# Token-major residual: down, output, v and embedding-gate products with 512 moving weight columns

## The chip, the cores and the metric

The kernel runs on one core of one Trainium2 chip. The metric is the device time of one execution in microseconds (us). TensorE (PE) multiplies; VectorE (DVE) and ScalarE (ACT) do elementwise work; GpSimd (POOL) does a few powers; SyncE (SP) issues most transfers from memory.

## The reference

256 tokens of width 1024 go through two blocks A and then two blocks B. A SwiGLU network has 2816 hidden columns. All arithmetic is fp32.

```
# block A, twice
h = h + 0.5 * swiglu(rmsnorm(h, g1), w_gate, w_up, w_down)
z = rmsnorm(h, g2) @ w_in          # MLA, differential attention, pooling, 3 gates
h = h + sum(sigmoid(z_gate) * (branches @ w_branch)) @ w_out
h = h + 0.5 * swiglu(rmsnorm(h, g3), w_gate, w_up, w_down)
# after both: h = rmsnorm(h, final_norm)
# block B, twice: each step ends in a norm of its own before the residual
h = h + rmsnorm(swiglu(rmsnorm(h, ..), ..), ln_ffn1_post)
h = h + rmsnorm([attention | mLSTM | RWKV](rmsnorm(h, ..)) @ w_out, ln_mix_post)
h = h + rmsnorm(swiglu(rmsnorm(h, ..), ..), ln_ffn2_post)
h = h + rmsnorm(sigmoid(rmsnorm(h, ..) @ w_ple_gate) * (ple @ w_ple_proj), ln_ple_post)
```

## The kernel before

The residual `x` is kept feature-major: 128 partitions of features, 8 chunks of them, 256 tokens. An fp32 product is made of three passes over operands split in two parts each (`hi`, `lo`): hi·hi, hi·lo and lo·hi (`mm3`, L330). The stationary operand is a 128x128 piece of weight, the moving one 256 columns of tokens. Gate and up (`mm2`, L337) take hi and lo of the activation as one moving operand of 512 columns and then 256 more. `weights` (L291) fetches a weight of 512 KB into one of four `raw` buffers in two pieces; ACT makes the hi part in slices of 128x512 (L449) and DVE the lo part (L450). The weights of the next stage are fetched and split "ahead" while the last down product runs.

An FFN (`ffn`, L688) walks over 11 groups of 256 hidden columns: gate, up, silu, product, split into `h`, and the down product of the group before into four PSUM banks `acc`. A norm at the start of a step (`Norm`, L509) doesn't scale the activation: it splits `x` times the gain into hi and lo (L452, L453), sums the squares with ACT, DVE and a product with ones (L422), takes a power -0.5 on POOL, spreads the factor over partitions with a matmul (L430), and the factor is multiplied in behind the products (`rb`). In A, `x` is updated bank by bank as the last down product's banks end (L776, L778). In B a norm lies between the product and the residual (`Post`, L586): the sum of squares over all features must be known before any of `x` can be updated, so `finish` (L641) comes after the last product: column sums (L601), the power, the spread, then the multiplies and adds chunk by chunk (L663, L666), each followed by the split for the next product. `warm` (L434) puts 7 and 8 bf16 matmuls of zeros (L438) beside this chain.

A scheduler orders the instructions of every engine from the program and modelled durations; `chain` (L311) pins a few of them one behind the other. Each engine runs its own list strictly in order. The lines of the profile:

```
L334 mm3: one of three passes, 256 moving columns     L341/L342 mm2: 512 and 256 columns
L449/L450 split of weights or h (ACT hi / DVE lo)      L452/L453 split of x times a gain
L438 warm   L430 spread   L422/L601 column sums        L415/L656 power on POOL
L663/L666 residual update in B   L776/L778 residual update in A   L1740, L1741, L1744 embedding gate
```

## Time and profile before

| | |
|---|---|
| median of 3 runs | 2453.72 us (2452.12 to 2458.3) |
| the profiled execution | 2454.61 us |
| its span | 2452.8 us |
| PE busy / DVE / ACT / POOL | 2401.3 / 1855.1 / 1474.5 / 43.6 us |
| mean granted clock of PE | 0.991 |

Busy time is the time in which an engine had an instruction under way. A matmul's duration contains the length of the pipeline, so that neighbours overlap: what one costs in a stream is the distance from its start to the next one's start, not its duration. All times below are on one axis that begins with the span. PEclk is the share of full speed that PE was granted in a stretch: 1.00 is 2.4 GHz, and a stretch that lies half at 1.2 GHz reads 0.75.

### The profile page before, as it was taken

What the parts mean: (1) busy time and instruction counts of PE and PEld (TensorE: products, weight loads), DVE (VectorE), ACT (ScalarE), POOL (GpSimd) and SP (SyncE); (2) the same over time, 40 slices, a digit from 0 to 9 for tenths busy, and PEclk for the clock granted to TensorE, in tenths of its full rate; (3) what the DMA queues carried; (4) which work ended last, traced back from release to release, by engine and by line L of the source; (5) the groups of instructions that cost most, each with busy time, mean ns of one, the idle gap of its engine ahead of it and who ended that gap; (6) DMA issues with size and microseconds to landing.
All of it is one profiled execution on the core that took longest, in us unless ns stands there. A gap on an engine that the chain in (4) does not pass through costs nothing. (4 is left out here: it accounts for less than half of the span.)

```text
span 2452.8 us, 45590 instructions
## 1 busy us (share of the span) xinstructions
PE 2401.3 (98%) x17164; PEld 2234.8 (91%) x17164; DVE 1855.1 (76%) x3620; ACT 1474.5 (60%) x2954; POOL 43.6 (2%) x43
## 2 busy tenths in 40 slices
PE   8999999999999999999999999999989999999998
PEld 7999999999999999999999988989989998898997
DVE  7667888767767888877787688777667768877765
ACT  6556765656656676566666663466666665346655
POOL 0000000000000000000000000000000000000000
PEclk9999999999999999999999999999999998999998
DMA  6554444555555444455555542156525554215651
GB/s 227 187 187 155 147 143 167 189 190 189 184 191 190 143 147 148 166 197 189 181 189 185 185 135 83 44 170 212 199 95 194 187 180 132 84 43 165 214 198 58
DMA packets 110510, 396.62 MB, mean 162 GB/s; under 512 B 12752, under 2 KB 13264, under 8 KB 110288
## 3 DMA queue, kind: packets, MB, share of 16 engines
q1 hardware_dynamic: 109008, 391.33, 47.7%
q8 instruction: 135, 2.21, 0.3%
q10 hardware_dynamic: 1280, 2.36, 0.3%
q14 instruction: 87, 0.71, 0.1%
HBM read 392.60 MB, written 1.05 MB: 160 GB/s over the span
## 5 line engine op out<-in xcount | busy, mean ns | idle before, releaser
L449 ACT ACTIVATE wh<-raw 128x512 fp32r<-128x512 f32 (+1 forms) x1446 | 891.6, 628 | 456.0 <-PE mm L334 120.0
L450 DVE TENSOR_TENSOR wl<-raw,wh 128x512 fp32r<-128x512 f32 (+1 forms) x1446 | 978.8, 688 | 239.5 <-ACT wh L449 218.6
L341 PE MATMUL mm<-act,wh 128*128 128x512 f32 x1728 | 613.2, 395 | 13.4 <-ACT wh L449 8.8
L342 PE MATMUL mm<-act,wl 128*128 128x256 f32 x1728 | 482.2, 280 | 0.7 <-DVE wl L450 0.7
L334 PE MATMUL acc<-h,wh 128*128 128x256 f32 x2560 | 457.0, 280 | 0.0
L334 PE MATMUL mm<-act,wh 128*128 128x256 f32 (+1 forms) x2176 | 422.5, 289 | 7.4 <-DVE sc L890 2.5
L341 PEld LDWEIGHTS mm<-act,wh 128*128 128x128 f32 x1728 | 324.3, 188 | 86.0 <-ACT wh L449 8.8
L334 PEld LDWEIGHTS acc<-h,wh 128*128 128x128 f32 x2560 | 391.2, 188 | 4.1 <-ACT h L449 0.3
L334 PE MATMUL acc<-h,wl 128*128 128x256 f32 x1280 | 355.8, 279 | 0.0
L334 PEld LDWEIGHTS mm<-act,wh 128*128 128x128 f32 (+1 forms) x2176 | 342.7, 190 | 13.9 <-ACT act L452 3.3
L342 PEld LDWEIGHTS mm<-act,wl 128*128 128x128 f32 x1728 | 326.2, 189 | 1.8 <-DVE wl L450 1.2
L334 PE MATMUL mm<-act,wl 128*128 128x256 f32 x1088 | 310.9, 287 | 0.0
L341 PE MATMUL up<-act,wh 128*128 128x512 f32 x832 | 296.0, 394 | 0.1
L334 PEld LDWEIGHTS acc<-h,wl 128*128 128x128 f32 x1280 | 240.5, 188 | 0.3
L342 PE MATMUL up<-act,wl 128*128 128x256 f32 x832 | 232.2, 279 | 0.0
L334 PEld LDWEIGHTS mm<-act,wl 128*128 128x128 f32 x1088 | 206.6, 190 | 2.6 <-issue 1.8
L341 PEld LDWEIGHTS up<-act,wh 128*128 128x128 f32 x832 | 155.9, 187 | 34.1 <-DVE uu L349 0.5
L342 PEld LDWEIGHTS up<-act,wl 128*128 128x128 f32 x832 | 156.8, 189 | 0.5
L348 ACT ACTIVATE jn<-mm 128x256 f32<-128x256 f32 x216 | 80.2, 372 | 88.7 <-PE mm L342 88.6
L743 ACT ACTIVATE ga<-ga 128x512 f32<-128x512 f32 x88 | 55.1, 630 | 100.6 <-DVE ga L742 100.6
L349 DVE TENSOR_TENSOR ga<-mm,jn 128x256 f32<-128x256 f32 x112 | 47.1, 421 | 65.8 <-ACT jn L348 65.8
L341 PE MATMUL acc<-act,wh 128*128 128x512 f32 x256 | 92.4, 401 | 1.9 <-ACT wh L449 1.9
(506 smaller groups left out, 3242.0 us busy)
## 6 DMA issues: line engine op xcount, KB each, us to landing
raw<-a_wgate SPq DMA_DIRECT2D x88, 512.0 KB, 4.3
raw<-a_wup SPq DMA_DIRECT2D x88, 512.0 KB, 4.0
raw<-a_wdown SPq DMA_DIRECT2D x88, 512.0 KB, 4.3
raw<-b_wgate SPq DMA_DIRECT2D x88, 512.0 KB, 4.6
raw<-b_wup SPq DMA_DIRECT2D x88, 512.0 KB, 4.5
raw<-b_wdown SPq DMA_DIRECT2D x88, 512.0 KB, 4.4
raw<-a_win SPq DMA_DIRECT2D x80, 512.0 KB, 3.7
raw<-a_wbr SPq DMA_DIRECT2D x24, 512.0 KB, 3.6
```

What stands on the lines that cost most here:

```text
L334: pin(s.nc.tensor.matmul(out, lhsT=w[x], rhs=a[:, y], start=start and i == 0, stop=stop and i == 2, skip_group_check=True))
L341: s.nc.tensor.matmul(bank, lhsT=hi, rhs=a.rearrange("p a t -> p (a t)"), start=start, stop=False, skip_group_check=True)
L342: s.nc.tensor.matmul(bank[:, :T], lhsT=lo, rhs=a[:, 0], start=False, stop=stop, skip_group_check=True)
L348: s.nc.scalar.activation(t, b[:, T:], AF.Copy)
L349: s.nc.vector.tensor_tensor(out[:, i], b[:, :T], t, op=ALU.add)
L449: pin(nc.scalar.activation(hi, src, AF.Copy))
L450: pin(nc.vector.tensor_tensor(lo, src, hi.bitcast(F32), op=ALU.subtract))
L743: nc.scalar.activation(ga, ga, AF.Silu)
```

## The change

`x` becomes token-major: 128 tokens on partitions, two halves, 1024 features. For down, both `w_out`, the v columns, the embedding gate and its projection the operands change places: 128 tokens of the activation are stationary, and 512 columns of weight (384 for the v columns of B) move (`yt`, `gemm_h`). The same holds for the first group of each FFN, whose gate and up weights now lie side by side in one 512-column weight; its `h` comes out token-major and is transposed back on PE. All other products are as before. For them the norm transposes `x` on PE, four 128x128 pieces to a PSUM bank, and splits each piece from PSUM (`Norm.cols`). Sums of squares are now along a row: one ACT instruction with an accumulator for each token half. The norm factor is a value per partition, so that the residual update is one DVE instruction per 512 columns. In B the gain is a tile `G` of 128 equal rows, fetched for each step. The last down product runs the four banks of half 0 and 1 in order of halves. `warm`, the column sums and the third weight fetched ahead go.

```diff
+    def yt(s, out, w, c, n, a, h, start, stop, pin=lambda i: i):
+        w = w.cols(c, n)
+        for i, (x, y) in enumerate(((0, 0), (1, 0), (0, 1))):
+            pin(s.nc.tensor.matmul(out, lhsT=a[:, y, h * P:h * P + P], rhs=w[x], start=start and i == 0, ...
+    def gemm_h(s, ws, act, tags, both=False):
+        for i in range(2 * 8):
+            h, k = (i % 2, i // 2) if both else (i // 8, i % 8)
+            w, p = parts[k]
+            s.yt(bs[h][:, :w.m], w, p * w.m, w.m, act[k], h, k == 0, k == 7)
 class Norm:
+    def cols(n, h, q):
+        b = s.ps(n.tags[q])
+        for i in range(4):
+            k = 4 * q + i
+            s.nc.tensor.transpose(b[:, i * P:(i + 1) * P], s.x[:, h, k * P:(k + 1) * P], s.c("ident"))
+        for i in range(4):
+            s.split(a[:, 0, ts], a[:, 1, ts], b[:, i * P:(i + 1) * P], n.gain[:, k:k + 1])
+    def square(n, h):
+        s.nc.scalar.activation(s.tile([P, D], "sj"), s.x[:, h], AF.Square, scale=D ** -0.5, accum_out=ss)
+    def factor(n, h):
+        n.power(n.r[:, h:h + 1], n.var[:, h:h + 1], n.square(h))
 class Post:
-        s.warm("up", 7)
-        rb = s.spread_ps(r, s.chain)
-            s.warm("up", 8)
+    def bank(p, h, q, y, half):
+        s.nc.scalar.activation(s.tile([P, D], "sj")[:, :512], y, AF.Square, scale=..., accum_out=p.ss[h][:, q:q + 1])
+        s.nc.vector.tensor_tensor(p.yg[h][:, c], y, p.G[:, c], op=ALU.mult)
+    def finish(p, h, eps, nxt, out=None):
+        nc.vector.scalar_tensor_tensor(v, ss[:, 0:1], eps ..., ss[:, 1:2], op0=ALU.add, op1=ALU.add)
+        nc.gpsimd.tensor_tensor(r, v, s.mhalf[:, :1], op=ALU.pow)
+        for q in range(2):
+            nc.vector.scalar_tensor_tensor(s.x[:, h, c], p.yg[h][:, c], r, s.x[:, h, c], op0=ALU.mult, op1=ALU.add)
+            if nxt is not None:
+                nxt.cols(h, q)
+        if nxt is not None:
+            nxt.factor(h)
 def ffn(...)
+        for hf, i, kk in ([(hf, i, kk) for hf in range(2) for i in range(2) for kk in range(2)] if last else
+                          [(hf, i, kk) for kk in range(2) for i in range(2) for hf in range(2)]):
+            s.yt(acc[hf][i], w, kk * D + i * 512, 512, h[:, kk], hf, j == 0 and kk == 0, last and kk == 1, ...
         if j == 0:
-            g, u, g2 = s.gemm2([wg[j], wu[j], wg[1]], act, ("mm", "mm", "acc", "acc", "acc", "acc"), ws=ws)
+            bs = s.gemm_h(ws or [s.weights([w])[0] for w in wgu], act, ("mm", "mm"), first)
+            for hf in range(2):
+                nc.scalar.activation(ga, bs[hf][:, :T], AF.Silu, scale=nrm.r[:, hf:hf + 1])
+                nc.vector.tensor_tensor(ht, bs[hf][:, T:], ga, op=ALU.mult)
+                for kk in range(2):
+                    nc.tensor.transpose(two(b)[:, kk, o], ht[:, kk * P:(kk + 1) * P], s.c("ident"))
+                s.split(h[:, :, 0, o], h[:, :, 1, o], two(b)[:, :, o])
 def mix_a(...)
+    for h, b in enumerate(s.gemm_h(ws, act, ("mm", "mm"))):
+        nc.scalar.activation(vd[:, h], b, AF.Copy, scale=nrm.r[:, h:h + 1])
```

How the instructions move is shown at three places. The first is PE's list at the end of the second FFN of A's first layer; before, the last down product (`dh`, `dl` are its weights) is followed by the gate product of the next FFN (`wh`, `wl`):

```order
L334 MATMUL acc_5905<-h_7647,dh_7734 128x256 x2
L334 MATMUL acc_5905<-h_7647,dl_7735 128x256
L341 MATMUL mm_7909<-act_7824,wh_7750 128x512 [waits DVE_49,PE_49]
L342 MATMUL mm_7909<-act_7824,wl_7751 128x256
L341 MATMUL mm_7910<-act_7824,wh_7750 128x512 [waits PE_49]
L342 MATMUL mm_7910<-act_7824,wl_7751 128x256
```

After, the same place (`st` and `up` are the PSUM banks that take the transposed `x`):

```order
L416 MATMUL acc_5505<-dh_7094,h_6906 128x512
L544 MATMUL st_7165<-cst_63,x_61 128x128 [waits DVE_49]
L544 MATMUL st_7165<-cst_63,x_61 128x128 x3
L544 MATMUL up_7180<-cst_63,x_61 128x128 [waits DVE_49]
L544 MATMUL up_7180<-cst_63,x_61 128x128 x3
L416 MATMUL mm_7243<-wh_7102,act_7170 128x512 [waits Activation_49]
L416 MATMUL mm_7243<-wl_7103,act_7170 128x512
L416 MATMUL mm_7243<-wh_7102,act_7170 128x512 [waits DVE_49]
L416 MATMUL mm_7243<-wh_7106,act_7170 128x512 [waits Activation_49]
```

Eight transposes of token half 0 stand between the last down product and the next stage's first, which waits for a split made from them; another eight, of half 1, stand further down among the products of half 0. The second place is ACT's list there; before, splits straight from `x` stand among the squares:

```order
L452 ACTIVATE act_7824<-x_61,vec_62 128x256 [waits DVE_49]
L452 ACTIVATE act_7824<-x_61,vec_62 128x256
L526 ACTIVATE sq_7829<-x_61 128x512
L452 ACTIVATE act_7824<-x_61,vec_62 128x256 [waits DVE_49]
L452 ACTIVATE act_7824<-x_61,vec_62 128x256
```

After, the same splits come from PSUM, in alternation between the two banks (`act_7170` and `act_7185` are the two halves of the features):

```order
L554 ACTIVATE sj_7195,v_1644_7194<-x_61 128x1024 [waits DVE_49]
L471 ACTIVATE act_7170<-st_7165,vec_62 128x128 [waits PE_49]
L554 ACTIVATE sj_7228,v_1648_7227<-x_61 128x1024 [waits DVE_49,Activation_49]
L471 ACTIVATE act_7185<-up_7180,vec_62 128x128 [waits PE_49]
L471 ACTIVATE act_7170<-st_7165,vec_62 128x128 [waits DVE_49]
L471 ACTIVATE act_7185<-up_7180,vec_62 128x128 [waits DVE_49]
```

The square of token half 1 stands behind the first split, and each later split waits for DVE's lo part of the one before from the same bank. The third place is PE's list at the end of the first FFN group of that next FFN, after the change (`jn` is the token-major product of silu(gate) and up; before there is no such transpose):

```order
L416 MATMUL mm_7244<-wl_7135,act_7185 128x512
L416 MATMUL mm_7244<-wh_7134,act_7185 128x512 [waits DVE_49]
L674 MATMUL up_7293<-cst_63,jn_7295 128x128 x2
L352 MATMUL mm_7337<-act_7170,wh_7320 128x512 [waits PE_49,Activation_49]
L674 MATMUL up_7293<-cst_63,jn_7303 128x128 [waits DVE_49]
L674 MATMUL up_7293<-cst_63,jn_7303 128x128
L353 MATMUL mm_7337<-act_7170,wl_7321 128x256 [waits DVE_49]
```

One product of the next group stands between the last product of half 1 and the transpose that needs its silu and multiply.

## Rows read from the trace of the kernel before

**Rows 1.** page: busy us (share of the span) and instructions of each engine

```profile
PE 2401.3 (98%) x17164; PEld 2234.8 (91%) x17164; DVE 1855.1 (76%) x3620; ACT 1474.5 (60%) x2954; POOL 43.6 (2%) x43
```

**Rows 2.** timeline of PE in A's first mixer: start us, us, what

```profile
242.03 0.28 PE L334 MATMUL mm<-act,wl 128*128 128x256 f32 x1
...
242.75 0.40 PE L377 MATMUL S<-wh,qm 128*128 128x512 f32 x1
...
243.45 0.28 PE L334 MATMUL mm<-act,wl 128*128 128x256 f32 x1
```

**Rows 3.** timeline of PE, A layer 1, first FFN to mixer

```profile
799.32 0.40 PE L334 MATMUL acc<-h,dh 128*128 128x256 f32 x2
...
805.07 0.51 PE L334 MATMUL mm<-act,wh 128*128 128x256 f32 x3
```

**Rows 4.** timeline of PE, A layer 0: the spread in its mixer

```profile
221.05 0.60 PE L430 MATMUL st<-cst,r 128*128 128x128 f32 x4
```

**Rows 5.** waits of PE over the whole span: us, times, longest

```profile
PE mm L334 <- DVE ud L1166: 3.4, 2, 1.9
PE mm L334 <- DVE sc L890: 2.5, 2, 1.2
```

**Rows 6.** groups of ACT by form: count, busy us, mean ns, idle before

```profile
L743 ACT ACTIVATE ga<-ga 128x512 f32<-128x512 f32 x88 | 55.1, 630 | 100.6 <-DVE ga L742 100.6
...
L861 ACT ACTIVATE pT<-PT 128x128 f32<-128x128 f32 x16 | 4.3, 270 | 2.0 <-PE PT L859 1.4 <-ACT sc L849 0.3
...
L946 ACT ACTIVATE qk<-row 32x1024 f32<-32x1024 f32 x4 | 4.0, 1048 | 0.0
```

**Rows 7.** groups of DVE by form

```profile
L666 DVE TENSOR_TENSOR x<-x,yg 128x512 f32<-128x512 f32 x24 | 16.5, 688 | 0.1
...
L1074 DVE SCALAR_TENSOR_TENSOR sc<-sc,rs 128x128 f32<-128x128 f32 x16 | 5.6, 349 | 0.1
...
L1072 DVE TENSOR_TENSOR rs<-rs,lam 128x1 f32<-128x1 f32 x32 | 5.0, 157 | 0.6
```

**Rows 8.** groups of POOL by form

```profile
L656 POOL TENSOR_TENSOR r<-v,mhalf 128x2 f32<-128x2 f32 x8 | 5.6, 697 | 745.7 <-DVE v L655 686.2 <-DVE v L653 59.5
```

**Rows 9.** timeline of PE, end of B's first FFN, layer 0

```profile
1408.45 0.28 PE L334 MATMUL acc<-h,dl 128*128 128x256 f32 x1
...
1414.26 0.80 PE L334 MATMUL mm<-act,wh 128*128 128x256 f32 x2
```

**Rows 10.** timeline of PE, end of B's mixer, layer 0

```profile
1594.92 0.28 PE L334 MATMUL accB<-act,wl 128*128 128x256 f32 x1
...
1601.48 0.50 PE L341 MATMUL mm<-act,wh 128*128 128x512 f32 x1 [1.63 <-DVE act L453]
```

**Rows 11.** timeline of PE, end of B's second FFN, layer 0

```profile
1790.05 0.95 PE L601 MATMUL st<-cst,sq 128*128 128x1 f32 x8
...
1791.98 0.48 PE L334 MATMUL mm<-pt,ph 128*128 128x256 f32 x2
...
1794.93 0.60 PE L430 MATMUL st<-cst,r 128*128 128x128 f32 x4
...
1797.25 0.50 PE L334 MATMUL mm<-act,wh 128*128 128x256 f32 x2 [0.84 <-ACT act L452]
```

**Rows 12.** timeline of PE, end of B's embedding gate, layer 0

```profile
1821.57 0.28 PE L334 MATMUL pgb<-act,wl 128*128 128x256 f32 x1
...
1834.60 0.50 PE L341 MATMUL mm<-act,wh 128*128 128x512 f32 x1 [1.52 <-DVE act L453]
```

**Rows 13.** timeline of PE at the end of the span

```profile
2436.48 0.28 PE L334 MATMUL pgb<-act,wl 128*128 128x256 f32 x1
```

**Rows 14.** timeline of DVE at the end of the span

```profile
2448.86 0.69 DVE L666 TENSOR_TENSOR x<-x,yg 128x512 f32<-128x512 f32 x1
```

**Rows 15.** two stretches: length, busy us of five engines, PEclk, DMA share, GB/s

```profile
219.00:225.00 6.00, 4.75 (x40) 4.53 (x39) 3.90 (x10) 3.55 (x8) 0.59 (x1) 1.00 0.56 170
1408.00:1416.00 8.00, 7.13 (x46) 5.69 (x45) 5.00 (x14) 4.28 (x11) 0.70 (x1) 0.79 0.28 87
```

More of the change, by code (lines that the diff above doesn't have):

```diff
@@ L95, in layout @@
     d["a_win"] = np.stack([_chunks(w[l][:, 416:], 256) for l in range(DEPTH)])
+    d["a_win_v"] = np.stack([_kchunks(w[l][:, 416 + 1024:416 + 1536], 4) for l in range(DEPTH)])
     uq = a["mla_w_uq"].reshape(DEPTH, 256, 8, 96)
@@ L579, in apply @@
-    def apply(n):
-        s = n.s
-        rb = s.spread(n.r1)
-        for k in range(8):
-            s.nc.vector.scalar_tensor_tensor(s.x[:, k], s.x[:, k], s.v(n.fin, k), rb, op0=ALU.mult, op1=ALU.mult)
-class Post:
-    ORDER = (6, 0, 1, 2, 3, 4, 5, 7)
-    def __init__(p, s, gain):
-        p.s, p.gain, p.yg, p.sq, p.sum, p.n = s, gain, [None] * 4, {}, None, 0
-        p.held = []
-    def total(p, sq, stop=False):
-        s = p.s
-        if p.sum is None:
-            p.sum = s.ps("st")
-        for h in range(2):
-            s.chain(s.nc.tensor.matmul(p.sum[:, h:h + 1], lhsT=sq[:, h * P:(h + 1) * P], rhs=s.c("ones", 0, 1),
-                                       start=p.n == 0 and h == 0, stop=stop, skip_group_check=True))
-        p.n += 1
-    def scale(p, o, bank):
-        s = p.s
-        if p.yg[o // 2] is None:
-            p.yg[o // 2] = s.t2("yg")
-        s.chain(s.nc.scalar.activation(p.yg[o // 2][:, o % 2], bank[:, o % 2], AF.Copy, scale=s.v(p.gain, o)))
-    def step(p, o, bank, late=False):
+        r, v = n.r[:, h:h + 1], n.var[:, h:h + 1]
@@ L1103, in _mix_a @@
     it = items()
-    for j in range(6):
+    for j in range(4):
         proj(j)
@@ L1108, in _mix_a @@
         gate(i)
-        for _ in range(2 if i < 6 else 1):
+        for _ in range(2 if i < 8 else 1):
             next(it, None)
@@ L1684, in ffn_b, with middle @@
     A = s.A
-    post = Post(s, f"b_f{f}o_{l}")
+    post = []
+    def middle():
+        post.append(Post(s, 4 * l + (1 if f == 1 else 3)))
+        if mid:
+            mid()
     er = s.tile([P, 2], "er")
     s.nc.vector.tensor_scalar(er, nrm.var, 4 * EPS, None, op0=ALU.mult)
-    ready = ffn(s, nrm, A[f"b_wgate{f}"][l], A[f"b_wup{f}"][l], A[f"b_wdown{f}"][l], post.step, ws, ahead, mid=mid)
+    acc, ready = ffn(s, nrm, A[f"b_wgu{f}"][l], A[f"b_wgate{f}"][l], A[f"b_wup{f}"][l], A[f"b_wdown{f}"][l], ws, ahead, middle)
     if fill:
         fill()
-    post.finish(er, 0.5, nxt)
+    for h in range(2):
+        for q in range(2):
+            post[0].bank(h, q, acc[h][q], 0.5)
+        post[0].finish(h, er, nxt)
     return ready
@@ L1708, in block_b @@
         m = Norm(s, f"b_pli_{l}")
[L1709 to L1719 removed]
+        with s.phase("pl", dict(pj=1), {}):
+            pj = s.tile([P, 2, D], "pj")
             def early():
@@ L1770, in program @@
         n = Norm(s, "a_ffn1_0")
-        for k in range(8):
-            n.tile(k)
-        def pre():
-            for b in range(4):
-                n.squares(b)
-            n.finish()
+        with s.phase("x0", dict(xT=2), {}):
+            xT = Wide(s, 8, "xT")
+            for k in range(0, 8, 2):
+                s.nc.scalar.dma_start(out=xT.pair(k // 2), in_=A["xT"][:, k:k + 2])
+                for i in range(k, k + 2):
+                    s.split(n.act[i][:, 0], n.act[i][:, 1], xT[i], n.gain[:, i:i + 1])
+        s.load()
+        for h in range(2):
+            n.factor(h)
         def tables():
```

507 lines of the change are left out of this document (205 added, 302 removed).

## The prediction

> **What bounds the kernel now.** I read the busy times first. PE is busy for 2401.3 of 2452.8 us, DVE for 76% and ACT for 60% [rows 1]: the kernel is one long list of products, and time can come only from products that get cheaper, from PE's waits, or from the work put on PE between products. So I next took the distance between neighbouring products in the timeline of PE, then the seams, the places at which one stage's last product hands over to the next stage's first. There the two blocks differ. In A the products run on: the last down products start at 799.32, the mixer's first product at 805.07 with no idle time noted beside it [rows 3]; the wait comes later in the mixer, for the norm's factor: the list of waits has it twice with 2.5 us in all (for `sc`), and 3.4 us for its like at the two starts of B's mixer (for `ud`) [rows 5]. In B a norm lies behind the product, and PE does nothing useful from 1408.57 (a product's cadence behind 1408.45) to 1414.26 [rows 9], 5.7 us; from 1595.04 to 1601.48 [rows 10], 6.4 us; from 1790.05 to 1791.98 and from 1794.93 to 1797.25 [rows 11], 4.3 us; from 1821.69 to 1834.60 [rows 12], 12.9 us; and behind 2436.6 up to the end of the span [rows 13], 16.2 us. All but the last two occur in both layers.
>
> **The products.** The down products turn 4224 products of 256 columns into 2112 of 512, and both output products, the embedding gate and its projection 1536 into 768: 2880 new ones for 5760 old, with the same columns in sum. (The v columns and the first FFN groups change too, but the first groups had 512 columns for two thirds of their work before, so I leave them out.) Six products of 256 columns take 242.75 - 242.03 = 0.72 us and the three of 512 that follow take 0.70 [rows 2]: 0.240 against 0.233 for the same columns. The 48 down products of rows 3 take 5.75 us, 0.2396 for two. So a pair saves some 0.006 us by these rows, which are read to 0.01 us; the three products of 512 could also cost 0.236 each, where nothing is saved, or 0.230. I take 0.0045, between: 2880 x 0.0045 = -13 us, bounds 0 and -18.
>
> The Trainium skill ("TensorE: Matmul & The Clock Gate", Part 2, back-to-back issue gap) gives columns over 2.4 GHz and 2.5 ns more, an estimate of 215.8 ns for 512 columns, and 131 ns for a sustained stream of them. The rows show 233 ns, so neither holds here for fp32 in reduced passes; by its constant alone a pair would save 2.5 ns, 7 us in all.
>
> **A's seams**, six of them (first FFN to mixer and mixer to second FFN in both layers, layer to layer, A to B). The order shows what now stands at one: eight transposes of half 0, then a product that waits for a split of them. The update of `x` for half 0 is done under half 1's 12 down products. A 128x128 transpose I take at 0.11 us, an estimate: four fp32 matmuls of that size take 0.60 us with the pipeline's length in it [rows 4], and eight narrow ones 0.95 [rows 11], which is 0.12 at most for one. Eight of them 0.9 us; the first split, 0.27 to 0.39 on ACT and 0.35 on DVE [rows 6, 7], partly under the second four: PE stands about 0.9 us. The square of half 1, 128x1024 on ACT, then holds the second split back by 1.05 us [rows 6], where the first piece's three products (0.70) cover part of what is then lost: about 0.6 more. Another eight transposes stand among the products, 0.9 us, and the spread and its handoffs 0.6. Sum 3.0 us; if every handoff comes late 3.7, if the splits keep ahead of PE 2.2. Before, the seam carries the column sums and the spread, 0.95 us (rows 4 and as much again for the sums), and at the two mixer starts the wait of 1.25 us, which goes, since the factor of each half is now known before the products end: 8.2 us in all. 6 x 3.0 - 8.2 = +10 us, bounds +5 and +14.
>
> **The first FFN group.** In the order, one product follows the last of half 1 before PE meets the transpose of `h`. That transpose waits for the silu of 128x256 (0.4, since 128x512 takes 0.63 [rows 6]) and a multiply (0.46, half way between the 0.35 of 128 columns and the 0.69 of 512 by columns [rows 7]), with two handoffs 1.1 us, less one product, 0.23; four transposes of `h` cost 0.44 more, all of it new. About 1.6 us, bounds 0.7 and 2.1. Behind PE's transpose everything of the second group is queued, so nothing covers this but the one product. Eight FFNs, of which the very first waits for its weights anyway: 7 x 1.6 = +11 us, bounds +5 and +15.
>
> **B's seams.** The chain of the norm now runs per half, and half 0's can run under half 1's products (12 x 0.233 = 2.8 us). For the half that ends last, what is left is a square of 512 columns (0.63, as the silu of that form), the variance (0.16) [rows 7], a power 0.70 [rows 8], two updates of `x` at 0.69 [rows 7], eight transposes and a split; half 0's first products stand before that and cover part. But the squares of `x`, the multiplies by G and the weights' splits share ACT's and DVE's lists with it, and behind the first FFN the next weights' splits stand behind the evacuation of the v products. Laid out by these durations I get: first FFN to mixer as long as before (0, twice), mixer to second FFN 0.5 less (twice, first group apart), second FFN to gate 1.3 less (twice; here the projection covers half 0), gate to first FFN 6.4 instead of 12.9 (once). The two waits of 1.7 us at the mixer's starts [rows 5] get shorter by about 1 each. Sum -1.0 - 2.6 - 6.5 - 2.0 = -12 us. If half 0's products cover all of half 1's chain, each of the six short seams is 3 us cheaper still (-30 in all); if the chain is cut up by the splits of weights, they are 2 us dearer (0).
>
> **The end.** Behind the last product: tanh 0.63, update of the gate 0.69, square 0.63 with its accumulator, a queue of one such square before it, variance 0.16, two powers 1.4, two updates 1.4, and 3.2 us from the last update to the end as now [rows 14]; some 8.2 against 16.2: -8 us, bounds -5 and -9.
>
> **Sum.** -13 + 10 + 11 - 12 - 8 = -12 us on the profiled execution's 2454.6, which is 2442.6. The median of the runs is 0.9 below that execution: 2442 us. Interiors of the mixers and the start (a second layout of `x` is loaded there) I take at 0, within 3.
>
> **The rivals.** *The seams are hidden.* The durations I laid out overlap in a stream, so the splits may keep ahead of PE everywhere: A +5, first group +5, B -30, columns and end as taken: -41, which I halve to -21 or so because both halves' chains still share two engines: 2433 down to 2413, in the middle 2422. For it: DVE at 76% and ACT at 60% have room; against it: they are busiest just at the seams.
>
> *Transposed norms pay at every seam* (slower). hi on ACT and lo on DVE read the same PSUM bank, and in the order each waits for the other. A step then costs 0.37 + 0.35 and two handoffs, about 0.85 us, against the 0.70 that PE needs for the three products. Over 16 steps that is 2.4 us for each of 13 norms, 31 us: 2473. It decides from 1.5 us per norm, 19 in all, from which on the sum is above +7. For it: the alternation in ACT's list. Against it: the two banks alternate, so a step can use the other bank's gap.
>
> *The columns save nothing* (512 at 0.236): +1 us, 2455, no change.
>
> *PE's clock.* With `warm` gone, PE idles at B's seams with transposes alone. In the stretch around the end of B's first FFN the granted clock is 0.79 on average even with it, while it stays at 1.00 in a stretch with one of A's waits of 1.25 us [rows 15]. 0.79 of 8 us means 3.4 us at the lower of the two levels, 1.2 GHz, which costs 1.7 us; at nine more seams than now that is +15: 2457, no change by a hair. The Trainium skill (the same page, Part 4) says that transposes don't count as busy for the gate in the same way, which speaks for this rival; rows 15 don't decide it, since there the idle time was filled with real matmuls.
>
> **How the numbers follow.** Chances: the forecast 0.45 (its own range 2433 to 2452), hidden seams 0.2, transposed norms slower 0.2, columns nothing 0.1, clock 0.05. No change means within 0.3%, 7.4 us, about what a measurement of this kernel can tell, 2446.4 to 2461.1. Of the forecast's 0.45 two thirds lie below 2446.4. Faster 0.3 + 0.2 = 0.5; same 0.15 + 0.1 + 0.05 = 0.3; slower 0.2. The range 2420 to 2464 leaves out the far half of either outer rival.
>
> **What would show it.** Right: 512-column products 0.230 to 0.235 us apart; no gap over 4 us at A's seams and 1 us or more before the transposes of `h`; 6 to 7 us at the gate's end; about 8 us behind the last product. Wrong: 512 columns at 0.236 or more; PE's idle time before L416 at each norm over 4 us with ACT or DVE splits as its cause; granted clock at 1.2 GHz behind each norm.

## The result, and the profile after

The changed kernel takes 2480.68 us, median of 4 runs (2480.24 to 2481.22), the kernel before beside it 2454.54: ratio 1.0105, interval 1.0088 to 1.0123. It is slower, where 2442 was forecast. The profiled execution has a span of 2478.5 us against 2452.8 and a mean granted clock of 0.987 against 0.991.

The page after, with the columns of [rows 1]:

```profile
PE 2394.0 (97%) x14020; PEld 2078.0 (84%) x14020; DVE 1804.1 (73%) x3592; ACT 1461.6 (59%) x2994; POOL 50.5 (2%) x66
```

PE has 3144 instructions fewer and is busy 7 us less, and still the span grew by 25.7 us: the time went into waits and into slower stretches. To find them I cut each trace at the starts of the stages' last products (f1 and f2 are the FFNs, pl the embedding gate) and subtracted. All numbers are us; the last two columns are experiments told below (e2 and e15):

```
              before   after   after-before    e2      e15
f1 A0         203.32   199.31     -4.0       198.93   197.40
mix+f2 A0     415.15   420.17     +5.0       419.66   418.55
f1 A1         186.47   188.85     +2.4       187.13   186.50
mix+f2 A1     416.31   426.18     +9.9       425.43   422.67
f1 B0         187.19   195.75     +8.6       197.82   192.53
mix B0        186.48   187.00     +0.5       185.79   189.19
f2 B0         192.12   193.59     +1.5       192.09   194.16
pl 0           34.53    39.61     +5.1        35.01    31.16
f1 B1         198.22   197.60     -0.6       195.23   192.07
mix B1        189.19   187.21     -2.0       186.22   185.98
f2 B1         192.95   193.79     +0.8       192.62   194.61
pl 1           34.54    39.43     +4.9        34.61    31.17
end            16.34     9.96     -6.4         9.95     9.95
```

**Pace of the products.** The timeline of PE in the changed kernel (start us, us, what), at the ends of runs of equal products: first of 64 gate and up products in A, first of 24 down products, first product behind; then the same 24 in B.

```profile
497.65 0.40 PE L352 MATMUL up<-act,wh 128*128 128x512 f32 x1
...
508.87 0.39 PE L416 MATMUL acc<-wh,h 128*128 128x512 f32 x1
...
514.31 0.40 PE L352 MATMUL mm<-act,wh 128*128 128x512 f32 x1
...
1284.87 0.39 PE L416 MATMUL acc<-wh,h 128*128 128x512 f32 x1
...
1290.47 0.40 PE L352 MATMUL mm<-act,wh 128*128 128x512 f32 x1
```

Down products: 5.44 / 24 = 226.7 ns in A (226.6 over longer runs) and 5.60 / 24 = 233.3 in B. But not in B's last groups, whose weights lie in tiles of their own (`dh`, `dl`): the last 12 products of one take 2.72 / 12 = 226.7 ns.

```profile
1427.55 0.62 PE L416 MATMUL acc<-dh,h 128*128 128x512 f32 x2
...
1430.27 0.39 PE L416 MATMUL acc<-dh,h 128*128 128x512 f32 x1
```

As the program is built, both operands start 32 bytes past a multiple of 64 in A. In B the stationary `h` starts at a multiple of 64, `wh` and `wl` 32 bytes past one, and `dh` and `dl` at one again.

Gate and up: 11.22 / 32 = 350.6 ns for a pair of 512 and 256 columns. The same in the kernel before, in A and at the start of its last FFN:

```profile
478.76 0.40 PE L341 MATMUL up<-act,wh 128*128 128x512 f32 x1
...
489.87 0.40 PE L334 MATMUL acc<-h,wh 128*128 128x256 f32 x2
...
2262.11 0.39 PE L341 MATMUL up<-act,wh 128*128 128x512 f32 x1
...
2273.41 0.41 PE L334 MATMUL acc<-h,wh 128*128 128x256 f32 x2
...
2279.02 0.40 PE L341 MATMUL mm<-act,wh 128*128 128x512 f32 x1
...
2290.12 0.40 PE L334 MATMUL acc<-h,wh 128*128 128x256 f32 x2
```

A pair takes 11.11 / 32 = 347 ns there, in one group 11.30 / 32 = 353, and 347 again in the next: one kernel, the same places in SBUF, two paces. Its first FFN has 353 throughout, the others 347. So these products, which the change doesn't touch, got 3.7 ns a pair slower.

**The gate's seam in B**, which answers to [rows 11]. PE in the changed kernel from the projection's last product on (in brackets the wait and what ended it):

```profile
1817.20 0.39 PE L416 MATMUL mm<-ph,pt 128*128 128x512 f32 x1
1821.12 1.11 PE L544 MATMUL st<-cst,x 128*128 128x128 f32 x4 [3.53 <-DVE act L472]
1822.03 1.06 PE L544 MATMUL up<-cst,x 128*128 128x128 f32 x4
1826.29 0.80 PE L416 MATMUL pgb<-wh,act 128*128 128x512 f32 x1 [3.20 <-DVE act L472]
1826.88 0.63 PE L416 MATMUL pgb<-wl,act 128*128 128x512 f32 x1
```

Two waits, both ended by splits. Half 1's transposes stand in PE's list ahead of half 0's first product and wait for half 0's last splits, which still read their bank `st`. The second wait isn't for data: all of half 0 was split before it, and the first product starts only behind the last split of half 1, on DVE, which it doesn't read:

```profile
1825.88 0.35 DVE L472 SCALAR_TENSOR_TENSOR act<-up,vec,act 128x128 fp32r<-128x128 f32 x1 [0.18 <-ACT act L471]
```

As the program is built, its output `pgb` takes the PSUM bank of `up`, out of which half 1 is being split. From 1817.20 to 1826.29 it is 9.1 us, where the kernel before needs 2.4 from its last projection product to its first product of the gate. Then the clock, with the columns of [rows 15]:

```profile
1821.00:1831.00 10.00, 6.68 (x20) 5.28 (x21) 3.06 (x11) 2.81 (x9) 0.00 (x0) 0.52 0.00 0
1831.00:1835.00 4.00, 4.00 (x19) 3.25 (x18) 0.12 (x1) 0.83 (x2) 0.00 (x0) 1.00 0.01 4
```

0.52 is the lower level, 1.2 GHz, nearly throughout: after PE had stood for 3.5 us, products start 0.43 us apart (1826.88 is the second, the third starts at 1827.31), where they take 0.23 at full clock.

**The seam from A to B.** ACT in the changed kernel, between the first and the last splits of the final norm:

```profile
1236.17 0.37 ACT L471 ACTIVATE act<-st,both 128x128 fp32r<-128x128 f32 x1
1237.36 1.06 ACT L554 ACTIVATE sj<-x 128x1024 f32<-128x1024 f32 x1 [0.82 <-DVE x L581]
...
1238.91 1.14 ACT L588 ACTIVATE x<-x,r 128x1024 f32<-128x1024 f32 x1
1239.96 1.05 ACT L554 ACTIVATE sj<-x 128x1024 f32<-128x1024 f32 x1
...
1241.77 0.37 ACT L471 ACTIVATE act<-up,both 128x128 fp32r<-128x128 f32 x1 [0.16 <-DVE act L472]
...
1244.56 0.37 ACT L471 ACTIVATE act<-st,both 128x128 fp32r<-128x128 f32 x1 [0.42 <-DVE act L472]
1245.34 0.37 ACT L471 ACTIVATE act<-st,both 128x128 fp32r<-128x128 f32 x1 [0.42 <-DVE act L472]
```

Two squares and the scaled copy, 3.3 us, stand in the list between half 0's splits, which PE waits for. The last two rows show the step of the splits where nothing else is in between: 0.78 us, ACT and DVE taking turns. PE's transposes of `x`, at this seam and at the one from A's layer 0 to layer 1, first of half 0 and last of half 1:

```profile
619.71 0.60 PE L544 MATMUL st<-cst,x 128*128 128x128 f32 x4
...
627.86 0.60 PE L544 MATMUL up<-cst,x 128*128 128x128 f32 x4
...
1234.74 0.60 PE L544 MATMUL st<-cst,x 128*128 128x128 f32 x4
...
1247.92 0.60 PE L544 MATMUL up<-cst,x 128*128 128x128 f32 x4
```

8.2 us there, 13.2 here. The granted clock is 0.51 from 1240 to 1247, so a part of the 13.2 is the lower clock: 512 columns take 0.43 us there.

**The first group**, layer 0 to layer 1: ACT, then PE.

```profile
634.59 0.47 ACT L670 ACTIVATE jn<-mm,nr 128x256 f32<-128x256 f32 x1 [2.47 <-PE mm L416]
...
635.23 1.15 ACT L468 ACTIVATE wh<-raw 128x512 fp32r<-128x512 f32 x2
```

```profile
635.91 0.50 PE L352 MATMUL mm<-act,wh 128*128 128x512 f32 x1 [1.20 <-ACT wh L468]
```

ACT stands 2.5 us for half 1's products, since the silu is next in its list; the second group's weight splits are queued behind it, and PE then waits for those. The transposes of `h` aren't what PE waits for. So it is in five of the seven FFNs; in B's first layer PE does stand 1.0 and 1.2 us at the transposes of half 1's `h` (at 1256 and 1637).

**A's second mixer**: PE, and a stretch with the columns of [rows 15].

```profile
1006.55 0.66 PE L1017 MATMUL PT<-cst,qm 128*128 128x128 f32 x4 [1.09 <-DVE qm L1013]
```

```profile
1008.00:1015.00 7.00, 6.40 (x30) 6.11 (x30) 2.51 (x6) 1.73 (x3) 0.00 (x0) 0.51 0.23 78
```

This wait and two more of 0.6 us behind it, for the splits of `qk`, are followed by 7 us at 1.2 GHz. The kernel before has no wait in this place, nor has the changed kernel in layer 0.

**The end of the gate**, the last product and the first of the next FFN:

```profile
1850.46 0.39 PE L416 MATMUL pgb<-wh,act 128*128 128x512 f32 x1
...
1857.49 0.80 PE L416 MATMUL mm<-wh,act 128*128 128x512 f32 x1 [0.19 <-ACT act L471]
```

From a cadence behind 1850.46 that is 6.8 us, where the kernel before needs 12.9 [rows 12]. The next products are again 0.43 us apart.

**The end**, which answers to [rows 13]: the last product starts at 2468.49, 10.0 us before the span's end.

### The profile page after: what moved, and what is told of

It is laid out like the page before. It is cut to its first block, busy times and chain, and to the rows that moved or that the text cites. A ratio compares the mean times of both kernels' runs of the same rounds, so it can differ in the third digit from the quotient of the medians.

```text
span 2478.5 us, 39114 instructions
## 1 busy us (share of the span) xinstructions
PE 2394.0 (97%) x14020; PEld 2078.0 (84%) x14020; DVE 1804.1 (73%) x3592; ACT 1461.6 (59%) x2994; POOL 50.5 (2%) x66
## 4 chain that ended last, share of the span: by engine, by line
PE 89%; DVE 4%; ACT 3%; DMA 1%; issue 1%; POOL 0%; ACTq 0%; DVEq 0%; POOLq 0%
PE acc L416 19%; PE mm L352 16%; PE mm L345 13%; PE up L352 8%; PE mm L353 8%; PE mm L416 6%; PE up L353 4%; PE S L345 2%; PE pgb L416 2%; DVE wl L469 1%; PE S L994 1%; PE PT L790 1%; PE accB L416 1%; PE S L416 1%; DVE x L618 1%
## 5 line engine op out<-in xcount | busy, mean ns | idle before, releaser
L469 DVE TENSOR_TENSOR wl<-raw,wh 128x512 fp32r<-128x512 f32 x1454 | 972.0, 684 | 253.4 <-ACT wh L468 244.4
L468 ACT ACTIVATE wh<-raw 128x512 fp32r<-128x512 f32 x1454 | 884.6, 625 | 393.1 <-PE mm L345 83.6
L416 PE MATMUL acc<-wh,h 128*128 128x512 f32 x1280 | 410.9, 392 | 0.0
L352 PEld LDWEIGHTS mm<-act,wh 128*128 128x128 f32 x1664 | 312.8, 188 | 78.1 <-ACT wh L468 7.2
L345 PE MATMUL mm<-act,wh 128*128 128x256 f32 x1760 | 342.6, 291 | 10.0 <-ACT wh L468 5.6
L345 PEld LDWEIGHTS mm<-act,wh 128*128 128x128 f32 x1760 | 277.8, 191 | 15.2 <-ACT wh L468 7.0
L416 PEld LDWEIGHTS acc<-wh,h 128*128 128x128 f32 x1280 | 239.3, 188 | 54.2
L416 PE MATMUL acc<-wl,h 128*128 128x512 f32 x640 | 251.1, 392 | 0.0
L416 PE MATMUL mm<-wh,act 128*128 128x512 f32 (+1 forms) x512 | 181.8, 416 | 22.1 <-ACT act L471 9.8
L416 PEld LDWEIGHTS mm<-wh,act 128*128 128x128 f32 x512 | 96.7, 193 | 57.7 <-ACT act L471 21.7
L416 PEld LDWEIGHTS acc<-wl,h 128*128 128x128 f32 x640 | 120.1, 188 | 23.9
```

The lines of the kernel that those rows point to most:

```text
L345: pin(s.nc.tensor.matmul(out, lhsT=w[x], rhs=a[:, y], start=start and i == 0, stop=stop and i == 2, skip_group_check=True))
L352: s.nc.tensor.matmul(bank, lhsT=hi, rhs=a.rearrange("p a t -> p (a t)"), start=start, stop=False, skip_group_check=True)
L416: pin(s.nc.tensor.matmul(out, lhsT=a[:, y, h * P:h * P + P], rhs=w[x], start=start and i == 0, stop=stop and i == 2, skip_group_check=True))
L468: pin(nc.scalar.activation(hi, src, AF.Copy))
L469: pin(nc.vector.tensor_tensor(lo, src, hi.bitcast(F32), op=ALU.subtract))
```

## The experiments

Each was timed in 5 rounds; ratios are to the kernel before, whose medians beside them lie between 2452.74 and 2453.5 (2454.54 beside the result), so a difference of two experiments' medians is good to some 2 us. Stages are read from one profiled execution of each kernel.

**e1: the gate's products first.** Half 1's transposes, splits and factor are issued behind half 0's gate products.

```
+            if mid and i == 8:      # behind half 0's eight products
+                mid()               # m.cols(1, 0), m.cols(1, 1), m.factor(1)
```

> Changed kernel, with one reordering: at both hand-overs from B's second FFN to the embedding gate the eight transposes, splits and norm factor of token half 1 are issued behind the gate's 24 products of half 0 instead of ahead of them. Theory 'order' (the loss at the seams is mostly PE standing at an instruction that waits, with ready products queued behind it): in the profile of the changed kernel PE stands 3.9 and 3.6 us at each of these two seams while half 0's input has long been there; both waits go except about 1 us, so 2 x 5 to 6 us, and the time is about 2469 to 2471. Theory 'work' (the loss is the transposes' own time on PE and the chain of splits): the same transposes and splits remain, at most 2 us, 2479 or more. Theory 'clock' (PE runs at 1.2 GHz at the seams since the filler matmuls are gone): the 10 us stretch at 1.2 GHz there remains unless the idle time goes; with it gone another 2 x 2 us, 2465.

2476.79 us (1.0089, 1.0076 to 1.0102): 4 us of the expected 10. PE in this kernel, last projection product and first of the gate:

```profile
1815.99 0.39 PE L416 MATMUL mm<-ph,pt 128*128 128x512 f32 x1
1820.44 0.79 PE L416 MATMUL pgb<-wh,act 128*128 128x512 f32 x1 [4.06 <-DVE act L477]
```

4.5 us in place of 9.1, but a wait stays, and with it the lower clock (0.79 for a first product): it ends with the last of half 0's splits out of `up`, whose bank `pgb` takes here too, and not with the first split, which the product reads. The order on PE was half of the matter; the bank is the rest, together with the lists of ACT and DVE, which set when it comes free.

**e2: half 1 of h later.** Its transposes and split are issued behind the second group's gate products, and half 1's first products use another bank.

```
-    turn = [2]
+    turn = [0]
...
-            bs = s.gemm_h(ws or [...], act, ("mm", "mm"), first)
+            bs = s.gemm_h(ws or [...], act, ("mm", "acc"), first)
...
+            if pend:
+                pend.pop()(1)       # transposes and split of h, half 1
```

> Changed kernel, with one reordering in each FFN: the two transposes of h of token half 1 are issued behind the gate products of the second group, and the first group's half 1 goes to another PSUM bank, so that nothing at the start of the second group waits for silu. Theory 'order': seven of the eight FFNs lose 1.2 to 1.5 us there now, because ACT stands idle for the silu while the weight splits of the second group are behind it in its list; most of it comes back, 7 to 10 us, about 2471 to 2474. Theory 'work': the same transposes remain, no change, 2480.

2461.15 us (1.0028, 1.0020 to 1.0037), 19.5 less, twice what was expected. By the stages, f1 A1 and the FFNs of B gain 1.2 to 2.4 each (f1 B0 apart, which lost 2.1), the two stages with A's mixers 0.5 and 0.8, and the two gate stages 4.6 and 4.8, which the expectation did not have. PE in this kernel, and DVE's last split of half 1:

```profile
1813.18 0.39 PE L416 MATMUL mm<-ph,pt 128*128 128x512 f32 x1
1817.10 0.66 PE L544 MATMUL st<-cst,x 128*128 128x128 f32 x4 [3.53 <-DVE act L472]
1817.62 0.73 PE L544 MATMUL up<-cst,x 128*128 128x128 f32 x4
1818.04 0.75 PE L416 MATMUL pgb<-wh,act 128*128 128x512 f32 x1
```

```profile
1821.60 0.35 DVE L472 SCALAR_TENSOR_TENSOR act<-up,vec,act 128x128 fp32r<-128x128 f32 x1 [0.43 <-ACT act L471]
```

The first wait is the same, the second is gone: half 0's first product no longer waits for half 1's splits, which end 3.9 us behind its start. ACT and DVE do half 0's splits in the same order as in the changed kernel. What the edit changed is a bank: an FFN now uses `acc` before `up`, and as the program is built `up` lies in another bank than the first `pgb`. So what the gate stages lost came for the most part from the bank that the two share in the changed kernel. No run changes the bank alone.

**e3: narrow columns.** All token-major products of 512 columns are issued as two of 256.

```
+            for e in range(2):
+                ... out[:, e * m:e * m + m], rhs=w[x][:, e * m:e * m + m] ...
```

> Changed kernel, with each product of 512 (384) moving weight columns issued as two products of 256 (192) with the same stationary operand; all else as before. Theory 'columns save little': by the cadences in the profiles (226.6 and 233.3 ns for 512 columns in A's and B's down products, 235.6 for two of 256 before) 1056 x 9 + 1056 x 2.3 = 12 us come back for down, some 3 for the others: about 2494 to 2497. Theory 'columns save nothing' (the gain is eaten inside the same stream): 2481, within 3 us. If the token-major form saves more than its cadence shows (fewer weight loads): above 2500.

2493.37 us (1.0163, 1.0150 to 1.0176), 12.7 more, a little less than expected: in sum the wide columns give what they were priced at. They don't give it evenly. In this trace the 48 narrow down products of a group take 239.4 ns a pair in A, against 226.6 for the wide one in the same place, and 233.3 in B, against 233.3: all of the gain is in A.

**e4: transposes twice.** Each transpose of `x` is issued twice.

```
+            for _ in range(2):
                 s.nc.tensor.transpose(b[:, i * P:(i + 1) * P], ...)
```

> Changed kernel, with each of the 208 transposes of x on PE issued twice into the same place. One transpose takes 0.109 us from start to start. Theory 'work' (PE's own time for the transposes is on the path): plus 208 x 0.11 = 23 us, about 2503. Theory 'order' (PE waits at the seams anyway): those of half 0 at the start of a seam add their time (8 per seam, 13 x 0.87 = 11 us), those of half 1 stand where PE partly waits, so plus 11 to 18 us, 2492 to 2498.

2499.08 us (1.0184, 1.0171 to 1.0197), 18.4 more, at the upper end of theory 'order' (11 to 18) and below the 23 of theory 'work': most of the transposes' own time lies on the path, but not all of it.

**e5: B's h moved by 32 bytes** (on e2).

```
+    s.nc.vector.memset(s.tile([P, 2], "pad"), 0.0)     # ahead of B's FFN tiles
```

> The kernel of the second experiment (second half's transposes of h behind the next group's gate products; 2461.15 us), and B's four FFNs get a tile of 32 bytes ahead of their others, so that h lies 32 bytes past a multiple of 64 there, as it does in A's FFNs; nothing else. In the changed kernel a pair of 512-column down products takes 2 x 226.6 ns in A's FFNs and 2 x 233.3 in B's. Theory A (where the stationary h lies sets the pace of the down products): B's fall to 226.6 ns, 4 FFNs x 384 products x 6.7 ns = 10 us less, of which what now waits behind takes some: 2451 to 2455. Theory B (the pace comes from something else that B's FFNs have): 233.3 stays, 2459 to 2463. By neither should the gate and up pair (350.7 ns) move, since its operands stay where they are.

2455.76 us (1.0011, 1.0002 to 1.0019), 5.4 less. (The expectation counted 384 products an FFN; it is 264, so 7.1 us.) The 24 down products of B:

```profile
1382.60 0.39 PE L416 MATMUL acc<-wh,h 128*128 128x512 f32 x1
...
1388.04 0.40 PE L352 MATMUL up<-act,wh 128*128 128x512 f32 x1
```

5.44 us in place of 5.60, A's pace. The start of the stationary operand sets it, but only as seen from the moving one: in B's last groups of the changed kernel `h` starts at a multiple of 64 bytes too, and with a moving operand that does the same the pace is 226.7 (rows at 1427.55).

**e6: everything 64 bytes further** (on e2).

```
-        s.mhalf = s.tile([P, 16], "mhalf")
+        s.mhalf = s.tile([P, 32], "mhalf")
```

> The kernel of the second experiment (2461.15 us) with one small constant tile 64 bytes longer, so that all tiles behind it lie 64 bytes further on; the normed x and the weights' splits are then at the offsets in 128 bytes that they have in the kernel before (32 instead of 96). A gate and up pair (512 and 256 columns) takes 350.7 ns in the changed kernel and 347 in seven of the eight FFNs of the kernel before. Theory A (the operands' place sets that pace): 347 in this run, 2560 pairs x 3.7 ns = 9 us less, 2450 to 2454. Theory B (not the place): 350.7 stays and the time is 2459 to 2463.

2462.15 us, and 350.7 ns a pair: theory B. Moving all tiles together changes nothing.

**e7: B's seams reordered** (on e2): half 1's squares and gain products behind half 0's last split, half 1's transposes and splits behind half 0's products.

```
+            if i == 8 and late and nrm.late:
+                nrm.late.pop()(s.last_yt)     # cols(1, q) and factor(1)
+        pin(s.nc.scalar.activation(... AF.Square ...))  # half 1: behind half 0's last split
```

> The kernel of the second experiment (2461.15 us) with B's seams put in another order: what token half 1 needs on ScalarE and VectorE (squares, gain products) is listed behind half 0's last split, and half 1's transposes, splits and factor are issued behind half 0's first products. Theory order (the seam's cost is that the two halves' work is interleaved in the in-order lists of ScalarE and VectorE, so that the first product waits for both): B's seven seams lose 1 to 3 us each, some 12 in all: 2447 to 2453, and the wait for a split of half 1 inside the first products is under 1 us. Theory volume (the 32 split steps of a norm at 0.7 to 0.8 us take the time, in whatever order, since half 0's products are only 3 us long for two weights of 1 part each and 12 for a whole half): the wait moves from ahead of half 0's products to ahead of half 1's and the time stays within 3 us, 2458 to 2464. Against both: half 1's work holds up the weights' splits queued behind it, slower, 2465 to 2475.

2462.78 us (1.0037, 1.0025 to 1.0050): the time of theory volume. The waits moved, as it said: in this list of waits the products of `acc`, which here are half 1's first ones, have a new entry.

```profile
PE pgb L416 <- DVE yg L627: 6.5, 2, 3.2
...
PE acc L416 <- ACT act L476: 4.8, 2, 2.4
```

At the gates the run doesn't decide between the theories. Half 0's splits are done 1.7 us before its first product starts, and that one waits for `yg`, a gain product of half 1, which reads `acc`: as the program is built, that bank is the one that `pgb` takes.

**e8: no final norm** (on e2).

```
-  ... else Final(s, "a_fin", "b_f1i_0")
+  ... else Norm(s, "b_f1i_0")
```

> The kernel of the second experiment (2461.15 us), and between A and B an ordinary norm in place of the final norm followed by B's first (this leaves out A's final norm with its second square, gain product and factors; nothing else). The first group behind that seam costs 8.2 us over an undisturbed one in the changed kernel, 2.0 in the kernel before, and 2.9 behind A's other second FFN. Theory A (the final norm's squares, products and factors stand in the in-order lists between the splits of half 0 and those of half 1): the seam falls to 3, 2455 to 2457. Theory B (the seam is dear because B's first weights or the gain rows' DMA come late there): it stays at 7 to 8, 2460 to 2462.

2459.01 us (1.0019, 1.0010 to 1.0029). The stage f1 B0 falls from 197.82 to 188.70, 9.1 us, which is theory A and more; the whole gains only 2.1, since the tiles moved too: in A's FFNs the down products take 233.3 ns here, which is 264 x 6.7 ns = 1.8 us an FFN, the mirror image of e5.

**e9: the weights' splits 1920 bytes further** (on e5).

```
-  s.tile([P, D], "sj")
+  s.tile([P, D + 480], "sj")[:, :D]
```

> The kernel of the fifth experiment (B's h moved by 32 bytes; 2455.76 us), with the scratch tile of the squares 1920 bytes longer, so that the weights' splits lie a multiple of 2048 bytes behind the normed x, as they do in the kernel before (49152 there, 53376 in the changed kernel). Theory A (how the moving and the stationary operand of the gate and up products lie to each other sets their pace): a pair of 512 and 256 columns takes 347 ns again instead of 350.7, 2560 pairs x 3.7 ns = 9 us, 2446 to 2449. Theory B (something else sets it): 350.7 stays, 2454 to 2458.

2463.91 us (1.0045, 1.0033 to 1.0058): slower by 8, against both theories. PE, the 64 gate and up products:

```profile
498.29 0.39 PE L352 MATMUL mm<-act,wh 128*128 128x512 f32 x1
...
509.58 0.40 PE L416 MATMUL acc<-wh,h 128*128 128x512 f32 x1
```

11.29 / 32 = 353 ns: the pace does follow the distance between the operands, but at the distance of the kernel before this kernel has that one's slow pace, not its fast one. The down products get slower too, 229.3 ns for 226.6, though their two operands moved together.

**e10 and e11: factors behind the splits** (on e5), in A, and in A and B.

```
             nxt.cols(h, q)
-        nxt.factor(h)
+    for h in range(2):
+        nxt.factor(h, nxt.pin)      # listed behind the last split of both halves
```

> The kernel of the fifth experiment (2455.76 us) with the factors of A's norms (the squares over 1024 elements, and in the final norm the gain product, the second square and the scaled copy) listed on ScalarE and VectorE behind the splits of both token halves, where they stood between the two halves' splits. Theory order (what stands between the splits holds up half 1's products at A's seams): the seam from A to B, 9 us dearer in B's first FFN than with an ordinary norm, gives 4 to 6 back, A's other five seams 0.5 to 1.5 each: 2445 to 2451. Theory volume (the same instructions are only late elsewhere, and the first group's factors now hold up its silu): within 2 us, 2454 to 2458; and slower, 2458 to 2462, if the weights' splits queued behind the squares come late for the next group.

> The kernel of the tenth experiment, with the same done at B's seams (both halves' factors behind both halves' splits there too). Theory order: B's seven seams with 10 us each give 1 us each more, 2438 to 2446. Theory volume: nothing more than the tenth gives, within 2 us of it. In B half 1's splits come later than half 0's by the whole square and gain work of half 1, so that half 0's factor may come late for its silu there: up to 1 us a seam slower than the tenth.

2453.25 (1.0004, 0.9994 to 1.0013) and 2451.99 us (0.9992, 0.9984 to 1.0001). PE at the seam from A to B in e10, the same two transposes as above:

```profile
1227.54 0.60 PE L552 MATMUL st<-cst,x 128*128 128x128 f32 x4
...
1234.74 0.60 PE L552 MATMUL up<-cst,x 128*128 128x128 f32 x4
```

7.2 us in place of 13.2, and f1 B0 3.9 shorter (the two profiled spans are 2459.2 and 2447.5 us, further apart than the medians, so a single stage is to be taken with some doubt). The medians give less than order theory asked for: 2.5 in e10, and 1.3 more in e11, which is what theory volume had for it. Each step alone lies within the noise, as the overlapping intervals show. The weights' splits, now behind the squares, hold up the second group by 1 us at a time. In B, e11 takes the gate stages to 31.1 (33.4 in e10) and gives 3.7 to 3.9 back in the second FFNs.

**e12, e14, e15: other distances** (on e11), and **e13: the kernel before, moved.**

```
e12:  mhalf [P, 32] and sj [P, D + 480]     e14:  sj [P, D + 224]     e15:  sj [P, D + 16]
e13 (kernel before):
-        s.mhalf = s.tile([P, 16], "mhalf")  # ahead of the normed x
+        s.mhalf = s.tile([P, 32], "mhalf")  # behind it
```

> The kernel of the eleventh experiment (2451.99 us), with the normed x and the weights' splits at exactly the places, in 2048 bytes, that they have in the kernel before (the 64 bytes of the sixth and the 1920 of the ninth experiment together). Theory A (their places set the pace of the gate and up products, and the ninth went the wrong way, 353.1 ns a pair, since it moved only one of them): 347 ns instead of 350.7, 9 us less, 2441 to 2445. Theory B (the distance alone counts, and zero is the slow one): 353.1 ns, 2456 to 2459. Theory C (what writes into SBUF beside the products counts, and not these places): 350.7, 2450 to 2454.

> The kernel before with one small constant tile allocated behind the normed x instead of ahead of it, and 64 bytes longer: normed x and weights' splits then lie, in 512 bytes, where they lie in the changed kernel, and 128 bytes more apart; each engine does the same work as before. Theory A (place): its gate and up pairs go from 347 ns to 350.7, 2560 x 3.7 ns = 9 us more, 2459 to 2463. Theory B (the place isn't it, the kernel before is faster there for another reason): 347 stays, 2451 to 2456.

> The kernel of the eleventh experiment (2451.99 us) with the weights' splits 896 bytes further from the normed x, so that the distance is a multiple of 1024 and not of 2048. If the distance counts in steps of 512 or 1024, this run has the ninth's pace (353.1 ns a pair, 2456 to 2459); if only in 2048, another one, 347 to 351 ns, 2442 to 2453; without any effect of place 350.7 and 2450 to 2454.

> The kernel of the eleventh experiment (2451.99 us) with the weights' splits 64 bytes further from the normed x (the distance is then 64 over a multiple of 128, where all kernels so far had a multiple of 128). If the pace follows the distance in 128 bytes, as the down products followed a shift of 32 bytes, it leaves 350.7 ns for another value, by up to the 6.7 ns seen there either way: 2435 to 2469; if 64 bytes count for nothing, 350.7 and 2450 to 2454.

```
      us       ratio (interval)           splits behind x, mod 2048   ns a pair   ns, 512-col down (A)
e12   2461.26  1.0036 (1.0023 to 1.0048)          0                     352.8         229.3
e14   2462.00  1.0040 (1.0026 to 1.0054)       1024                     352.8         229.3
e11   2451.99  0.9992 (0.9984 to 1.0001)        128                     350.7         226.6
e15   2447.78  0.9978 (0.9969 to 0.9987)        192                     349.1         227.9
e13   2456.91  1.0016 (1.0008 to 1.0025)        128                     351.3         (256 columns)
```

PE in e13 and in e15, 64 gate and up products each:

```profile
494.41 0.40 PE L339 MATMUL mm<-act,wh 128*128 128x512 f32 x1
...
505.65 0.40 PE L332 MATMUL acc<-h,wh 128*128 128x256 f32 x2
```

```profile
510.89 0.40 PE L352 MATMUL mm<-act,wh 128*128 128x512 f32 x1
...
522.06 0.39 PE L416 MATMUL acc<-wh,h 128*128 128x512 f32 x1
```

e13 settles it for the pace: the kernel before, doing the same work, goes from 347 to 351 ns a pair when its tiles lie where the changed kernel has them. It gets 4 us slower, about half of the 9 expected; the rest is open. e12 speaks against the absolute place, e14 against a distance that counts only in 2048 bytes (a weight's split is used in pieces of 128 columns, 512 bytes apart, so that multiples of 512 occur in any case). e15 is faster than both kernels, by 33 us than the changed one and 0.2% than the one before.

## Why the prediction was wrong

- **The products: right.** -13 was forecast. The down products give 4 x 264 x (226.6 - 235.6) = -9.5 us in A and 4 x 264 x (233.3 - 235.6) = -2.4 in B, -11.9 in all, against 2112 x 4.5 ns = -9.5. e3 has 12.7 for the columns of all token-major products. That A and B differ is a matter of place (e5), and what the width is worth hangs on the place too: 12.8 ns a pair in A's, nothing in B's (e3).
- **What the change leaves alone: wrong by 7.5 us.** The gate and up products were in no term. 2240 pairs got some 3.8 ns slower and the 320 of the first FFN 2.4 faster: +7.5 us. e13 shows that the pace comes from the place. New tiles (`sj`, `nr`, `nv`) moved the operands.
- **A's seams and first groups: half of them right.** With products and pace taken out, f1 A1 lost 3.6 us where one seam and one first group had been given 3.3, and mix+f2 A0 6.2 where it was 4.9. Twice it was more. A to B lost 7.9 for 3.3: I took the final norm for a norm, and its squares and its copy stand between the splits (rows above, e8, e10), some 2.6 of the loss being the lower clock behind these waits, an estimate that is worked out below. And mix+f2 A1 lost 11.1 for 4.9, some 6 of it inside A's second mixer, which the forecast took at 0: three waits of 2.3 us in all, and about 3 us, by the same estimate, for 7 us at 1.2 GHz behind them. Why ACT and DVE come late there, in layer 1 alone, stays open.
- **The first group's mechanism was wrong** in five of seven FFNs. The size, 1.6 us each, was near (its terms, 1.1 - 0.23 + 0.44, add up to 1.3), but PE waits for weight splits behind a silu in ACT's list, not for the transposes of `h`, which it waits for only in B's first layer. e2 takes half 1's transposes out of the way, the wait for weight splits goes, and f1 A1 and B's FFNs (f1 B0 apart) gain 1.2 to 2.4, A's second FFNs less.
- **B's seams: the step that failed most.** "Second FFN to gate 1.3 less (twice; here the projection covers half 0)": it is 5.1 and 4.9 us more, 12.6 off. The projection does cover half 0's transposes, but not its 16 splits, which take turns on ACT and DVE with half 1's squares and gain products. PE has half 1's transposes next in its list, and the gate's first product then waits for half 1's last split, since its output takes the bank that these splits read. The forecast had no term for a PSUM bank. Without that wait (e2) 4.6 and 4.8 of the 5.1 and 4.9 are gone; with the factors behind the splits as well (e11) the stages are 3.5 us shorter than in the kernel before, though the second FFNs give that back. "Gate to first FFN 6.4 instead of 12.9": the gap came, 6.8, but the stage behind it gained only 0.6 us, 1.3 with the pace taken out, where -6.5 and +1.6 had been laid out. The products behind the gap run at the lower clock, some 2.4 us by the estimate; the rest is not traced. The other seams of B came out near the forecast (mixers +0.5 and -2.0, second FFNs +0.8 and +0.2 with the pace taken out).
- **The end: -6.4 for -8**, inside its bounds (its terms add up to 8.7 us, not 8.2; it took 10.0).

These are 7.5, 4.6, 6.2, 12.6, 3.6 and 1.6, 36 of the 38 us between -12 and +26.

Of the rivals, the transposed norms that "pay at every seam" (2473) came nearest: a step of 0.78 us against the 0.85 supposed and the 0.70 that PE needs. But they don't pay alike at every seam; they pay where other work of ACT or DVE stands between the splits. The clock's rival holds in part: both gate stages of the changed kernel run their first products at 1.2 GHz for 10 us, behind waits of 3.5 and 3.2 us, and so do the products behind the gate, at the seam from A to B and in A's second mixer for 7 us each. In all, 58 us between the first full clock and the last product lie at 1.2 GHz, for 31 before. With 0.43 us for 512 columns in place of 0.23, and narrower products in proportion, the products in these stretches lose an estimated 21 us, for 12 before. These 9 us, of the 15 that the rival had, are contained in the items above. In these places the clock falls behind waits that have other causes, and makes them dearer. The Trainium skill ("TensorE: Matmul & The Clock Gate", Part 1) has the clock fall when the array stands idle; the rows of the gate's seam agree.

## What to carry to other kernels

When a step's consumers move from one wide operation to many small ones, read not only how long these take but what stands between them in each engine's list: here 3 us of squares between splits cost more than all transposes of a norm. A change that adds a few small tiles moves every operand behind them: compare the pace of the products that it doesn't touch, over long runs, before looking for reasons elsewhere. And where half a seam's work is put under the other half's products, check that the products come first in TensorE's own list, and that their output takes no PSUM bank which the other half's work still reads.

## What the runs showed of the hardware

The pace of back-to-back fp32 products depends on where the operands lie in SBUF, by up to 3%: 226.6 or 233.3 ns for 512 columns as the stationary operand starts 32 or 0 bytes past a multiple of 64 and the moving one 32 (e5, e8), 226.7 where both start at 0; 347 to 353 ns for a pair of 512 and 256 as the distance between moving and stationary tile changes (e9, e12 to e15). At one distance two paces are stable, and the kernel before goes from one to the other between two groups (2262 and 2279 us above); what chooses between them stayed open, and so did why the down products take 229.3 or 227.9 ns in e9, e12, e14 and e15. The Trainium skill ("SBUF — State Buffer", section "SBUF: two separate sides") says that TensorE's port waits for no other engine; whether these paces are a matter of ports no run here shows, but they aren't free of place.
